# W_out times the gate: made as hi and lo during the second half's projections and kept in DRAM

## The chip, the cores and the metric

The kernel runs on one core of a Trainium2 chip. The metric is the device time of one execution, in microseconds (us). The core's engines work from queues of their own, each in order: TensorE (PE, matrix products), VectorE (DVE), ScalarE (ACT), GpSimd (POOL) and SyncE (SP), which in this kernel issues every transfer between DRAM and on-chip memory (DMA).

## The reference

One layer on a sequence of 2048 rows with 1024 columns, all in float32. A product with `w_in` feeds two groups of heads: 4 heads of 128 with a gated delta rule (DeltaNet, "dn"), and 8 heads of 64 with attention over three dilated windows ("at"). Their outputs, each with its own norm and gate, stand side by side and go through one output product:

```python
mod = jax.nn.silu(c) @ w_mod[layer] + b_mod[layer]
shift, scale, gate = jnp.split(mod, 3, axis=-1)
h = rmsnorm(x, norm_w[layer]) * (1.0 + scale[:, None]) + shift[:, None]
proj = h @ w_in[layer]
...
mix = jnp.concatenate([o_dn, o_at], axis=-1) @ w_out[layer]
x = x + gate[:, None] * mix
return rmsnorm(x, final_norm_w)
```

The gate is one row of 1024 numbers for the whole sequence (there is one `c`), so the kernel multiplies the columns of `w_out` by it once, and not the product.

## The kernel before, in words

**Products.** PE multiplies in a shorter float format (float32r), so each operand is split: `hi` is the value rounded to that format, `lo` the rest. A product is three matmuls, hi by hi, hi by lo and lo by hi; each is recorded at line 149 (L149), and transposes at L154. To make a pair, ACT casts to hi, and POOL or DVE subtracts hi from the value to get lo.

**Stages.** The sequence is worked on in two halves. In each, the projections (16 units of columns of `w_in`, whose hi and lo are kept in the DRAM tiles `ws` after the first use and loaded back as 1 MB transfers, `w_hi<-ws` and `w_lo<-ws`) run on PE, and the DeltaNet scan, the convolutions and rotary terms run beside them. In the second half `gate_row` also works out the gate's row: 16 loads `wg` of 128x512, each added on DVE into `gacc`; the row goes to the DRAM tile `gscr`, which is complete at about 785 us. The projections end at about 1075 us. Then the attention runs, four pairs of heads (p = 0 to 3) with four blocks each, until about 1480 us; the last pair's blocks begin near 1393 us. The rest is the tail of the output product.

**The output product** takes rows 0 to 511 of `w_out` (for the DeltaNet heads' outputs) in three places: `mix_first`, four tiles of 128 rows between the projections and the attention (tiles `mf_oc`, `mf_hi`, `mf_lo`, `mf_x`; the result, `x` plus the product, is stored as `yscr<-mf_x`), and `mix_dn`, the other twelve, as filling between attention blocks (`m_x`). Rows 512 to 1023 (for the attention's outputs) are used by `mix_at`, 16 tiles, in the last pair and the tail.

**The weights of it** are made where they are used. `load_w` loads eight raw pieces of 128x512 and multiplies each by the gate's row, loaded from `gscr`; `split_w` makes hi and lo of them in the tiles of the pool `wp`, which has two slots for hi and two for lo, shared with the projections' `w_hi` and `w_lo`. Two k-tiles of 128 rows fit in one slot, so there are two pairs of tiles for a half of `w_out`, w[0] and w[1]. For the first half this happens in `first_keys`, at the last unit of the second half's projections: all multiplies on DVE (tile `wo_raw`), the gate's row in a piece of `q_lo`. For the second half it is begun in `pair_blocks`, at block 1 of the last pair by the program's numbering (raw pieces in `y_lo`, the gate's row in `y_hi`, DVE and POOL taking turns), and ended by `mix_at`, which waits until all eight are there, and before its first tile also waits for the attention's combined outputs.

**The order.** Generators stand in queues (`side`, `inv`, `dbl`, `scan`, `tail`, `late`, `aux`), and `tick` lets each take one step between the main program's steps; `hop(n)` lets n times 1.1 us of counted PE time go by. Work in `aux`, which holds `gate_row`, is the last in turn. A compiler then orders each engine's queue. The pool `t512` has 9 slots (T5) of 128x512 for small tiles of the projections, `wo_raw`, `z_at` and `wg` among them. The attention's own tiles: `sta` and `stb` are cleared by DVE first, `sm` is the masked scores, `p` the exponents, `pts` their transposes, `va` and `vb` the values, `po` the product with them, `ob` a copy of it by ACT at the end of a block.

## Time and profile before

| | |
|---|---|
| time, median of 3 runs | 1573.51 us (1571.19 to 1579.99) |
| time of the profiled execution | 1573.77 us |
| its span | 1571.5 us |
| granted TensorE clock, mean | 0.974 |
| PE busy | 1439.0 us, 92% |
| DVE busy | 1085.6 us, 69% |
| ACT busy | 655.0 us, 42% |
| POOL busy | 467.7 us, 30% |
| moved by DMA | 252.89 MB, 161 GB/s |

Times in rows count from the span's start. The span is what the trace covers; the execution's own time is 2.3 us longer. A granted clock of 1 is TensorE's upper level, 2.4 GHz. An idle time in square brackets stands before the instruction, with the work whose end released it; a wait for several things is put down to the one that came last, and where that one had long been done it was another. "Landing" is the time from a DMA's issue to its last byte.

### The profile page before, as it was taken

The page shows a single profiled execution, that of the slowest core. Times are in us where ns is not written, and L with a number is a line of the kernel's source. Part 1 is how long each engine was busy: PE and PEld are TensorE (multiplying, and loading weights), DVE is VectorE, ACT ScalarE, POOL GpSimd, SP SyncE. Part 2 cuts the span into 40 slices and gives each one's busy share as a digit, 9 for nine tenths or more (in the row PEclk, how much of TensorE's full clock was granted, in tenths as well). Part 3 has the DMA queues.
Part 4 walks back from the last instruction along what each step waited for, and adds up shares of the span by engine and source line. Part 5 has one row for each costly group of instructions (what it writes and reads, how often), then busy time and mean ns, then how long its engine had stood idle before and what let it go on. Part 6 is the DMA issues. An engine that isn't in the chain of part 4 may idle for free. (4 is left out here: it accounts for less than half of the span.)

```text
span 1571.5 us, 28399 instructions
## 1 busy us (share of the span) xinstructions
PE 1439.0 (92%) x9848; PEld 1162.1 (74%) x9848; DVE 1085.6 (69%) x3395; ACT 655.0 (42%) x1862; POOL 467.7 (30%) x573
## 2 busy tenths in 40 slices
PE   3898899889989879999999999997899999999997
PEld 2686778767767768877878788886677777777776
DVE  6868735775775875687877767435477777888766
ACT  3434224334324663423333243122355554567444
POOL 2324252353362333132141320213122212142243
PEclk9999999999999999999999999999999999999999
DMA  8845551743471652273542515437787747363364
GB/s 243 277 134 190 156 177 58 226 136 125 159 232 47 222 164 88 79 222 113 177 142 88 169 51 156 141 112 238 238 230 209 204 119 233 92 196 103 105 224 161
DMA packets 255183, 252.89 MB, mean 161 GB/s; under 512 B 44864, under 2 KB 196544, under 8 KB 254528
## 3 DMA queue, kind: packets, MB, share of 16 engines
q1 hardware_dynamic: 252592, 242.69, 50.0%
q10 hardware_dynamic: 2448, 8.39, 1.4%
q8 instruction: 78, 1.28, 0.3%
q14 instruction: 65, 0.53, 0.1%
HBM read 160.12 MB, written 90.90 MB: 160 GB/s over the span
## 5 line engine op out<-in xcount | busy, mean ns | idle before, releaser
L149 PE MATMUL ip<-h_hi,w_hi 128*128 128x512 f32 x864 | 353.4, 411 | 2.6 <-DVE gz L690 1.6
L149 PE MATMUL ip<-h_hi,w_lo 128*128 128x512 f32 x864 | 353.8, 411 | 0.0
L149 PE MATMUL ip<-h_lo,w_hi 128*128 128x512 f32 x864 | 351.9, 409 | 0.0
L149 PEld LDWEIGHTS ip<-h_hi,w_hi 128*128 128x128 f32 x864 | 165.3, 191 | 35.0 <-DVE gz L690 2.1
L149 PEld LDWEIGHTS ip<-h_hi,w_lo 128*128 128x128 f32 x864 | 165.5, 192 | 32.1 <-issue 0.2
L149 PEld LDWEIGHTS ip<-h_lo,w_hi 128*128 128x128 f32 x864 | 165.1, 191 | 31.8 <-issue 0.2
L677 DVE SCALAR_TENSOR_TENSOR cv_y<-cv_r,cw,cv_y 128x512 f32<-128x512 f32 x144 | 118.2, 821 | 37.9 <-ACT cv_y L674 34.4
L563 POOL TENSOR_TENSOR w_lo<-w_raw,w_hi 128x512 fp32r<-128x512 f32 x72 | 96.1, 1347 | 123.7 <-ACT w_hi L562 85.3
L1210 DVE CUSTOM_DVE_ANT_0 sm<-s,mask 128x256 f32<-128x256 f32 (+3 forms) x256 | 108.0, 447 | 17.6 <-PE s L149 10.9
L154 PE MATMUL tr<-cst,p 128*128 128x128 f32 x568 | 94.6, 287 | 6.8 <-ACT p L1213 5.3
L1235 DVE COPY pts<-tr 128x512 f32<-128x512 f32 (+1 forms) x120 | 73.1, 616 | 33.8 <-PE tr L154 33.0
L1213 ACT ACTIVATE p<-sm,stb 128x128 f32<-128x128 f32 (+3 forms) x128 | 70.9, 555 | 49.6 <-DVE stb L1210 37.4
L1213 ACT ACTIVATE p<-sm,sta 128x256 f32<-128x256 f32 (+1 forms) x128 | 63.2, 495 | 66.9 <-DVE sta L1210 59.7
L154 PEld LDWEIGHTS tr<-cst,p 128*128 128x128 f32 x568 | 61.8, 142 | 28.6 <-issue 17.1
L149 PE MATMUL ip<-w_hi,h_hi 128*128 128x264 f32 (+1 forms) x256 | 76.2, 298 | 4.8 <-DVE rp L1017 2.1
L791 DVE TENSOR_TENSOR tmp_inv<-xt_inv,blk 128x8 f32<-128x8 f32 (+14 forms) x240 | 73.2, 305 | 5.9
L149 PE MATMUL ip<-w_hi,h_lo 128*128 128x264 f32 (+1 forms) x256 | 75.7, 296 | 0.0
L149 PE MATMUL ip<-w_lo,h_hi 128*128 128x264 f32 (+1 forms) x256 | 75.6, 295 | 0.0
L679 ACT ACTIVATE cv_t<-cv_y 128x512 f32<-128x512 f32 x48 | 30.3, 632 | 86.1 <-DVE cv_y L677 77.0
L562 ACT CAST w_hi<-w_raw 128x512 fp32r<-128x512 f32 x72 | 43.6, 619 | 45.7 <-DMA w_raw<-in_w_in_dram 27.0
L1025 POOL TENSOR_TENSOR rp<-rx,tab 128x512 f32<-128x512 f32 x32 | 42.5, 1339 | 60.8 <-ACT rx L1015 47.1
L1037 POOL TENSOR_TENSOR r_lo<-rpc,r_hi 128x512 fp32r<-128x512 f32 x32 | 42.4, 1325 | 50.6 <-ACT r_hi L1036 28.3
(465 smaller groups left out, 3373.8 us busy)
## 6 DMA issues: line engine op xcount, KB each, us to landing
w_raw<-in_w_in_dram SPq DMA_DIRECT2D x72, 256.0 KB, 3.8
ws<-w_hi SPq DMA_DIRECT2D x15, 1024.0 KB, 5.5
ws<-w_lo SPq DMA_DIRECT2D x15, 1024.0 KB, 7.1
w_hi<-ws SPq DMA_DIRECT2D x15, 1024.0 KB, 5.8
w_lo<-ws SPq DMA_DIRECT2D x15, 1024.0 KB, 7.3
xt<-in_x_dram SPq DMA_DIRECT2D x16, 512.0 KB, 4.8
wm<-in_w_mod_dram SPq DMA_DIRECT2D x32, 256.0 KB, 5.6
tab<-ctab SPq DMA_DIRECT2D x32, 256.0 KB, 3.7
```

Source lines behind the costliest of these rows:

```text
L149: i = self.engine.matmul(ps, lhsT=lhsT, rhs=rhs, **k)
L154: i = self.engine.transpose(*a)
L562: A.copy(hi[:, s, 0:256], raw)
L563: G.tensor_tensor(lo[:, s, 0:256], raw, hi[:, s, 0:256], OP.subtract)
L677: V.scalar_tensor_tensor(y, r[:, n:n + J], cw[:, ti, n:n + 1], y, op0=OP.mult, op1=OP.add)
L679: A.activation(t, y, AF.Tanh)
L791: V.tensor_tensor(tmp[:, :, 0:i + 1], xt[:, :, 0:i + 1], b3[:, i:i + 1, 0:i + 1].to_broadcast([P, 4, i + 1]), OP.mult)
L1025: G.tensor_tensor(p2, xs[1 - ct], tab[1], OP.mult)
L1037: G.tensor_tensor(lo, pc, hi, OP.subtract)
L1210: V.tensor_tensor_reduce(out=sm, in0=pp[hd], in1=masks, scale=-0.125, scalar=BIG, op0=OP.add, op1=OP.min, accum_out=st[:, slot, hd:hd + 1])
L1213: A.activation(pt, sm, AF.Exp, scale=-1.0, bias=st[:, slot, hd:hd + 1], accum_out=st[:, slot, 2 + hd:3 + hd])
L1235: V.tensor_copy(pts[:, 0:kn], pt[:, 0:kn])
```

## The change

`make_w` is put into `aux` behind `gate_row`, so it begins after 785 us. For each of 16 pieces of `w_out` (all of it, both halves) it loads the raw piece and the piece of the gate's row, multiplies on DVE, casts on ACT, subtracts on POOL, and stores hi and lo into eight new DRAM tiles of 1 MB (`wos`). Between these are `hop`s of 4 (WLAG), 4 and 8 (WGAP), and all four of its tiles come from the nine slots of `t512`. `load_w` is now two loads of 1 MB for each pair of tiles. `first_keys` lets the queues step on until the first half is made, issues the loads of w[0], and those of w[1] later; `mix_at` loads the second half. The parts in `first_keys` and `pair_blocks` that loaded, multiplied and split go.

```diff
@@ -60,8 +60,8 @@
 PO = 1
 VD = 1
 VB = 5
-WLAG = 0.5
-GP = (0, 1)
+WLAG = 4.0
+WGAP = 8.0
 CMB = 4
 SMB = 3
 VAB = 3
@@ -272,6 +272,7 @@
     gscr = dram.tile([P, D], F32, name="gscr")
     oscr = [dram.tile([4, P, 4, J], F32, name=f"oscr{i}") for i in range(2)]
     yscr = dram.tile([4, J, D], F32, name="yscr")
+    oscr_w = [[dram.tile([P, 2, D], F32, name=f"wos{i}_{a}") for a in range(2)] for i in range(4)]
 
     def rsqrt(pool, y, a, tag):
 
@@ -1069,29 +1070,36 @@
         drain(aux)
 
 
-    def load_w(raws, ksel, grow, new, lag=0):
-
-        for j in range(8):
-            raw = new(j)
-            c = slice(j % 2 * J, j % 2 * J + J)
-            k = ksel + j // 2
-            dma(raw, w_out[k * P:(k + 1) * P, c])
-            if lag:
-                yield from hop(lag)
-            (G if lag and GP[j % len(GP)] else V).tensor_tensor(raw, raw, grow[:, c], OP.mult)
-            raws.append(raw)
-
-    def split_w(w, raws):
-
-        for i in range(2):
+    made = [0]
+
+    def make_w(pool):
+
+        for i in range(4):
+            for j in range(4):
+                new = lambda nm, dt=F32: pool.tile([P, J], dt, name=nm, tag="t512", bufs=T5)
+                k, c = 2 * i + j // 2, slice(j % 2 * J, j % 2 * J + J)
+                raw, g = new("wo_raw"), new("wo_g")
+                dma(raw, w_out[k * P:(k + 1) * P, c])
+                dma(g, gscr[:, c])
+                yield from hop(WLAG)
+                V.tensor_tensor(raw, raw, g, OP.mult)
+                hi, lo = new("wo_hi", F32R), new("wo_lo", F32R)
+                A.copy(hi, raw)
+                G.tensor_tensor(lo, raw, hi, OP.subtract)
+                yield from hop(WLAG)
+                for a, t in enumerate((hi, lo)):
+                    dma(oscr_w[i][a][:, j // 2, c], t.bitcast(F32))
+                yield from hop(WGAP)
+            made[0] += 1
+
+    def load_w(w, i0):
+
+        for i in range(i0, i0 + 2):
             w.append([flat(wp.tile([P, KT, 264], F32R, name=f"w_{nm}"))[:, 0:2 * D].rearrange("p (k d) -> p k d", k=2)
                       for nm in ("hi", "lo")])
-            for j in range(4):
-                raw = raws[4 * i + j]
-                hi, lo = (w[i][a][:, j // 2, j % 2 * J:j % 2 * J + J] for a in range(2))
-                A.copy(hi, raw)
-                (V if j % 2 else G).tensor_tensor(lo, raw, hi, OP.subtract)
-                yield i
+            for a in range(2):
+                dma(w[-1][a].bitcast(F32), oscr_w[i][a])
+            yield
 
     def class_rows(t, d):
 
@@ -1143,7 +1151,7 @@
 
             yield from mix(hi, lo, oc, w, use)
 
-    w, wa, raws = [], [], []
+    w, wa = [], []
 
 
     def stack(dst, scr, p, hd, step, j0, n):
@@ -1310,8 +1318,6 @@
                 else:
                     ya, yb = ahead["y"] = [hp.tile([P, 4, D], F32, name=f"y_{nm}", tag=f"h_{nm}", bufs=2)
                                            for nm in ("hi", "lo")]
-                    dma(ya[:, 0], gscr)
-                    aux.append(load_w(raws, 4, ya[:, 0], lambda j: yb[:, j // 2, j % 2 * J:j % 2 * J + J], WLAG))
             if blk and p < 3:
                 ahead["load"](blk - 1, blk)
             elif p and blk == 0:
@@ -1454,6 +1460,7 @@
             run(dn_unit(fa, h, js, hs, gts[half], launch, None if half or h else (wv, kqs)))
             if half == 1 and h == 0:
                 aux.append(gate_row(fa))
+                aux.append(make_w(fa))
             if h == 0:
                 ordered[0] = OD == 3
 
@@ -1472,13 +1479,10 @@
         drain(late)
         if jj == 0:
             t = [hp.tile([P, 4, D], F32, name=f"q_{nm}", tag=f"h_{nm}", bufs=2) for nm in ("hi", "lo")]
-            dma(t[1][:, 2], gscr)
-            wr = []
-            for _ in load_w(wr, 0, t[1][:, 2], lambda j: fa.tile([P, J], F32, name="wo_raw", tag="t512", bufs=T5)):
-                pass
-            ahead["w"] = split_w(w, wr)
-            for j in range(4):
-                next(ahead["w"])
+            while made[0] < 2:
+                tick()
+            ahead["w"] = load_w(w, 0)
+            next(ahead["w"])
             ahead["m"] = mix_first(fa)
             next(ahead["m"])
             ahead["q"] = load_q(t, 0, 0)
@@ -1555,9 +1559,7 @@
                 while "y" not in ahead:
                     yield
                 ya, yb = ahead["y"]
-                while len(raws) < 8:
-                    yield
-                yield from split_w(wa, raws)
+                yield from load_w(wa, 2)
                 fw = yb[:, 0]
                 bcast_row(fw, final_w, D)
                 yield from hop(MIXLAG2)
```

How it moves the work, in the compiled order of three places. First DVE, from the end of the projections (`z_at` is the last unit's output, `rs_u` and `rs_o` a norm of the scan) to the attention's first instruction, before:

```order
L1093 TENSOR_TENSOR w_lo<-wo_raw,w_hi 128x512
L282 SCALAR_TENSOR_TENSOR rs_u<-rs_u,so 128x4
L690 SCALAR_TENSOR_TENSOR z_at<-z_t,ip 128x512
L283 SCALAR_TENSOR_TENSOR rs_o<-rs_u,rs_o 128x4
L1093 TENSOR_TENSOR w_lo<-wo_raw,w_hi 128x512
L1141 TENSOR_TENSOR mf_x<-ip,mf_x 128x512 x4
L905 SCALAR_TENSOR_TENSOR oc<-tr,nwz,g 128x512
L1141 TENSOR_TENSOR mf_x<-ip,mf_x 128x512 x4
L1327 MEMSET sta 128x16
```

and after:

```order
L691 SCALAR_TENSOR_TENSOR z_at<-z_t,ip 128x512
L1149 TENSOR_TENSOR mf_x<-ip,mf_x 128x512 x4
L906 SCALAR_TENSOR_TENSOR oc<-tr,nwz,g 128x512
L1149 TENSOR_TENSOR mf_x<-ip,mf_x 128x512 x2
L1085 TENSOR_TENSOR wo_raw<-wo_raw,wo_g 128x512
L1149 TENSOR_TENSOR mf_x<-ip,mf_x 128x512 x2
L1085 TENSOR_TENSOR wo_raw<-wo_raw,wo_g 128x512
L1333 MEMSET sta 128x16
L1334 MEMSET stb 128x16
```

The subtractions are gone, and two of the making's 16 multiplies stand among the `mf_x`, the last of them right ahead of `sta`.

Second, SP's queue at the start of the attention. Before, behind the last two stores of `mf_x` and two pairs of `k` loads (of which the first row here is the end):

```order
L1153 DMA k_lo<-kscr_80 128x1x512
L1188 DMA va<-vscr 32x4x128 x4
L1190 DMA vb<-vscr 128x4x128
L1153 DMA q<-qscr_82 128x1x512 x2
L1188 DMA va<-vscr 32x4x128 x4
L1190 DMA vb<-vscr 128x4x128
```

After, from the last store of `mf_x` on:

```order
L1150 DMA yscr<-mf_x 128x512
L1082 DMA wo_raw<-in_w_out_dram 128x512
L1083 DMA wo_g<-gscr 128x512
L1161 DMA k_hi<-kscr_80 128x1x512
L1161 DMA k_lo<-kscr_80 128x1x512
```

and, behind another pair of `k`:

```order
L1091 DMA wos3_0_130<-wo_hi_11931 128x512
L1091 DMA wos3_1_131<-wo_lo_11932 128x512
L1161 DMA q_11959<-qscr0_82 128x1x512
L1161 DMA q_11960<-qscr0_82 128x1x512
L1161 DMA k_lo_12199<-kscr0_80 128x1x512
L1196 DMA va_11952<-vscr_117 32x4x128 x4
L1198 DMA vb_11953<-vscr_117 128x4x128
```

The load of the last raw piece comes behind the last store of `mf_x`, and the last two stores of the making, of tile `wos3`, ahead of `q`, `va` and `vb`.

Third, SP's queue around the first blocks of the last pair. Before:

```order
L1313 DMA y_hi<-gscr 128x1024
L1153 DMA q<-qscr_83 128x1x512
L1188 DMA va<-vscr 32x4x128 x2
L1078 DMA y_lo<-in_w_out_dram 128x512 x3
L1190 DMA vb<-vscr 128x4x128 x2
L1078 DMA y_lo<-in_w_out_dram 128x512
L1296 DMA oscr_122<-a_oc 512x1x128
L1250 DMA agz<-zscr 128x4x128
L1078 DMA y_lo<-in_w_out_dram 128x512 x2
L1253 DMA sscr<-sta 128x16
```

After, some two blocks earlier in the program, at the end of the pair before:

```order
L1101 DMA w_lo<-wos_1_129 128x2048
L1258 DMA agz<-zscr 128x4x128
L1304 DMA oscr_122<-a_oc 512x1x128
L1554 DMA yscr<-m_x 128x512
L1196 DMA va<-vscr 32x4x128 x4
L1261 DMA sscr<-sta 128x16
L1101 DMA w_hi<-wos_0_128 128x2048
L1161 DMA q<-qscr_83 128x1x512 x2
L1263 DMA stc<-sscr 32x4x4 x4
L1101 DMA w_hi<-wos_0_130 128x2048
L1101 DMA w_lo<-wos_1_131 128x2048
```

The eight loads of 256 KB and the gate's row became four loads of 1 MB, and these moved ahead by about two blocks. PE's order in the second half's projections is as before; twelve matmuls of `mix_at` moved from the tail in among the last pair's blocks.

## Rows read from the trace of the kernel before

**Rows 1.** Stretches: length, PE, PEld, DVE, ACT, POOL busy; clock, DMA share, GB/s.

```profile
783.00:1060.00 277.00, 272.38 (x2026) 222.00 (x2025) 174.23 (x549) 86.43 (x261) 67.65 (x110) 1.00 0.38 122
1070.00:1080.00 10.00, 4.18 (x19) 2.81 (x17) 9.83 (x17) 4.35 (x10) 4.88 (x5) 0.91 0.78 255
1080.00:1090.00 10.00, 8.48 (x27) 6.53 (x28) 5.09 (x11) 1.62 (x3) 4.65 (x4) 0.74 0.57 158
1380.00:1400.00 20.00, 19.39 (x183) 15.06 (x181) 18.94 (x67) 14.23 (x42) 7.86 (x8) 1.00 0.63 190
```

**Rows 2.** Tile wg, 600 to 800 us: ns min/median/max; DVE's idle time.

```profile
L337 DVE SCALAR_TENSOR_TENSOR gacc<-wg,sc,gacc x14: 698/750/1732, 682.6 to 764.9; 128x512 f32<-128x512 f32 x14
...
  DMA wg<-in_w_mod_dram: 5.2, 3
```

**Rows 3.** PE's timeline at the boundary: start us, us, instruction.

```profile
1074.51 0.40 PE L149 MATMUL ip<-h_lo,w_hi 128*128 128x512 f32 x1
1074.74 0.40 PE L149 MATMUL ip<-h_hi,w_lo 128*128 128x512 f32 x1
...
1083.01 0.63 PE L149 MATMUL ip<-w_hi,mf_lo 128*128 128x512 f32 x1
1083.44 0.63 PE L149 MATMUL ip<-w_hi,mf_hi 128*128 128x512 f32 x1
```

**Rows 4.** PE's waits, 1055 to 1125 us: us in total, times, longest.

```profile
PE ip L149 <- DVE rs_u L282: 5.6, 1, 5.6
...
PE po L149 <- DMA va<-vscr: 2.0, 1, 2.0
PE s L149 <- DVE sta L1327: 1.5, 1, 1.5
...
PE sc L149 <- ACT y L138: 1.0, 1, 1.0
```

**Rows 5.** DVE's timeline: start us, us, instruction, [idle before it <- releaser].

```profile
1081.66 0.68 DVE L690 SCALAR_TENSOR_TENSOR z_at<-z_t,ip 128x512 f32<-128x512 f32 x1
...
1085.80 0.69 DVE L1141 TENSOR_TENSOR mf_x<-ip,mf_x 128x512 f32<-128x512 f32 x1 [2.03 <-PE ip L149]
...
1112.48 0.69 DVE L1141 TENSOR_TENSOR mf_x<-ip,mf_x 128x512 f32<-128x512 f32 x1 [2.93 <-DMA mf_x<-in_x_dram]
1113.12 0.07 DVE L1327 MEMSET sta<- 128x16 f32 x1
```

**Rows 6.** The page: DMA issues, KB each, median us to landing.

```profile
w_hi<-ws SPq DMA_DIRECT2D x15, 1024.0 KB, 5.8
w_lo<-ws SPq DMA_DIRECT2D x15, 1024.0 KB, 7.3
```

**Rows 7.** Tile wo_raw: ns min/median/max, first and last start; landing of its DMAs.

```profile
L1081 DVE TENSOR_TENSOR wo_raw<-wo_raw,q_lo x8: 676/686/1770, 1067.3 to 1075.8; 128x512 f32<-128x512 f32 x8
...
L1093 POOL TENSOR_TENSOR w_lo<-wo_raw,w_hi x4: 1262/1398/1622, 1068.7 to 1081.9; 128x512 fp32r<-128x512 f32 x4
...
DMA to landing us min/median/max: 3.8/4.9/5.8
```

**Rows 8.** The timeline of SP's queue: start us, us, DMA, count.

```profile
1116.11 2.02 SPq L1188 DMA_DIRECT2D va<-vscr  x4
```

**Rows 9.** PE's timeline: the first products with va.

```profile
1122.38 1.96 PE L149 MATMUL po<-pts,va 128*64 128x128 f32 x18 [1.97 <-DMA va<-vscr]
```

**Rows 10.** One stretch, tile y_lo alone: DVE, ACT, POOL busy (instructions).

```profile
1388.00:1412.00 24.00, 5.81 (x6) 4.64 (x8) 10.81 (x8) 0.87 0.76 240
```

**Rows 11.** ACT's timeline: the copies that end the blocks of the last pair.

```profile
1393.28 0.56 ACT L1368 COPY ob<-po 128x512 f32<-128x512 f32 x1
...
1412.62 0.59 ACT L1368 COPY ob<-po 128x512 f32<-128x512 f32 x1 [1.15 <-PE po L149]
...
1429.21 0.58 ACT L1368 COPY ob<-po 128x512 f32<-128x512 f32 x1
```

**Rows 12.** DMA from 1048 to 1122 us: packets, bytes, mean.

```profile
DMA packets 13472, 15.81 MB, mean 214 GB/s; under 512 B 977, under 2 KB 7631, under 8 KB 13467
```

## The prediction

> **What bounds the kernel now.** I read the busy shares first (the table above: TensorE, PE, far ahead of VectorE, DVE), so work on other engines counts only where PE then waits; then the stretches, then the waits inside three of them. By stretches [rows 1], the second half's projections, 783 to 1060 us, leave PE 4.6 of 277 us idle, while DVE is idle for 103. The boundary to the attention, 1070 to 1080, is turned round: DVE 9.83 of 10 us busy, PE 4.18. At 1380 to 1400, in the attention, both are nearly full (19.39 and 18.94 of 20). The change takes work out of the two tight places and puts it into the loose one; what it leaves at the tight ones decides.
>
> **The loose stretch.** Each of 16 steps loads a raw 128x512 piece and a piece of the gate row, multiplies on DVE, casts on ScalarE (ACT), subtracts on GpSimd (POOL), and stores hi and lo. Engines serve their queues in order, so a multiply whose piece is late holds all that is behind it on DVE, and a store whose POOL result is late holds all later loads on SyncE's queue (SP). The nearest row is the gate row's own sum: 16 loads of the same size, each consumed by a DVE instruction and DVE idle for them 5.2 us in 3 waits [rows 2]. A step here has two such loads, so 10.4 us if in proportion and if all of it reached PE; nothing if DVE's 103 idle us swallow it. I take a quarter, **+2.6 (0 to +10.4)**: in the old run PE idled only 4.6 us in a stretch where DVE idled 103. The 16 casts and subtractions lie under PE's work there: should that cover fail, DVE's 16 multiplies at 0.69 us would be 11 us.
>
> A row to weigh: a gacc of one form takes 0.75 us at the median and 1.73 at most [rows 2]. The Trainium skill (SBUF — State Buffer, Who interferes with whom) says that a DVE instruction with two inputs in SBUF contends with a GpSimd instruction that reads it, and one of them blocks; the change puts all 16 subtractions on GpSimd. By that the worst is 16 times 0.98 = 15.7 us of DVE time more, an estimate from that row; with a quarter of it on PE, as above, the sum at the end would be 1582 instead of 1578. The row's median of 0.75 shows the long form to be the exception, so I leave it out of the sum and give it 0.03 of A's chance of slower.
>
> **The boundary up to the last mf_x.** The last projection matmul ends at 1075.1 [rows 3]; PE had waited 1.0 us for an ACT y, and then waits 5.6 us for a PSUM bank [rows 4]. The profile calls the releaser rs_u, but the banks are freed by the last two z_at on DVE, the later at 1081.66 [rows 5], queued behind multiplies of W_out and w_lo subtractions. With these gone, the 1.0 us goes. The 5.6 does not go whole: the second pair of loaded weights, w[1], reuses the slot of the last projection's weights, so its hi is issued only at that unit's end, T, and its lo behind the store of the last z_at (I take T+2.1: two z_at of 0.68 and a store issue). A 1 MB load of this form lands in 5.8 (hi) and 7.3 us (lo) [rows 6], so T+5.8 and T+9.4. PE can run 12 matmuls on w[0] before, at 0.43 us spacing at the lower clock level or 0.23 at the full one [rows 3]; at 1080 to 1090 the granted clock is 0.74 [rows 1]; then it waits for w[1]. Its other 12 end at T+12.2 to T+14.6, while in the old run the two mf_x of the first tile start with 1085.80 [rows 5], T+10.7. So the first tile is about even, the earlier T gives 1, and a little comes from lighter DVE and ACT: **-1.5**. Lower end -3, if the wait is filled and the ten slow-clock matmuls (10 x 0.20 us) become fast. Upper end +4: lo issued only at T+6.5, where the last z_at was before.
>
> The loads of 1 MB deserve a word. The row gives 5.8 and 7.3 us. The Trainium skill (SBUF — State Buffer, The DMA setup-cost knee) has a fixed 2 us and 436 GB/s, hence 4.4 us for 1 MB and 2.6 for 256 KB, an estimate from its fit, and advises the largest transfers, which speaks for this change. By it w[1] would be 2.9 us earlier and the whole sum lower by that, 1575; the trace has 256 KB landing in 4.9 here [rows 7], so I stay with the rows.
>
> **The start of the attention.** Here I see the loss. The steps of the making do not all end before the projections: in the changed order the last two multiplies stand among the first W_out tiles, the two before them in the last head's scan. The last one's raw load is on SP right behind the store of the last mf_x, its multiply right before the memset of sta, the attention's first DVE instruction, and its store of lo stands before q and va. In the old trace the last mf_x starts at 1112.48, and the memset follows at 1113.12 without a gap [rows 5]. Now call Y the end of the last mf_x: the load is issued at Y+0.5, lands 3.8 to 5.8 us later [rows 7], and takes 0.69 to be multiplied: sta comes at Y+5.0 to Y+7.0 instead of Y. PE waits for sta already (1.5 us, [rows 4]). Then the cast on ACT and the POOL subtraction (1.3 to 1.6 us, [rows 7]) hold the store of lo to about Y+8.5, and behind it stand q, a k_lo and four va. The old SP put the four va out from 1116.11 on [rows 8], some 3 us after Y, and PE, which waited 2.0 us for them [rows 4], began with them at 1122.38 [rows 9]: Y+9.2, 4.3 us after the last was issued. The new SP needs from Y+8.5 some 2 us for the store, q and k, 2.0 for the va, and with 4.3 as before the po matmuls start near Y+16.8: 7.6 later. The two delays overlap. Scores and transposes of the first block fill little of it, because they depend on the DVE that is late too. **+6.5 (+5.0 to +12)**: the upper end is the va delay with landings of 5.8 throughout and with k and q late as well.
>
> **Last pair of heads.** Before, eight raw pieces are loaded, multiplied, cast and subtracted during the blocks around 1388 to 1412; on DVE this is 5.81 us [rows 10]. Its first block ends at 1412.62, 19.34 us after 1393.28; the next, without such work, takes 16.59 [rows 11]. The work removed is thus worth 2.75: **-2.8**, lower end -5.8 (DVE is full, all of it counts), upper end 0 (see D). What it leaves is the DVE's own attention work, which is then the last.
> In its place four loads of 1 MB now stand on SP some 30 us earlier, in front of q and va loads of the pair before. A load behind one can be late by its 7.3 us [rows 6] less the 3 or so that it takes alone: **+1 (0 to +4)**. Where PE has scores of another block in hand, it hides this.
> **Tail.** Twelve of the W_out matmuls of the tail get in among the attention's, 12 x 0.23 = 2.8 us if PE had idle time for them there; I take half, **-1.5 (-2.8 to 0)**: PE has few gaps at 1380 to 1400.
>
> **The sum**: 2.6 - 1.5 + 6.5 - 2.8 + 1.0 - 1.5 = +4.3. The profiled execution took 1573.77 us, 0.26 from the median of the runs, 1573.51; so 1573.8 + 4.3 = 1578.1, I say **1578**.
>
> **Rivals.**
> A, the forecast, 1571 to 1586, chance 0.50.
> B, faster: the old wait before W_out, DVE's load in the last pair and the tail pay in full (-3, -5.8, -2.8), the loose stretch costs nothing, and the start of the attention is late only by part of what the order shows, +1.5, because PE had W_out tiles to finish meanwhile: 1573.8 - 10.1 = 1563.7. For it speaks the 5.6 us gap and DVE's full 10 us; against it, that the multiply before sta waits for a load issued after the last tile. 0.13.
> C, slower: traffic. Between 1048 and 1122 the queue moves 15.81 MB at a mean of 214 GB/s [rows 12]; at 1070 to 1080, where the transfers crowd, 255 [rows 1]. The change brings 4 MB of loaded weights and four steps of 1 MB here, and takes 2.5 MB away: +5.5 MB. At 255 GB/s that is 21.6 us, against a room of 74 us x (255 - 214) = 3.0 MB or 11.9 us. So 9.7 us are not hidden, and mf_x's operands, k and va land late by that: 1578.1 + 9.7 = 1587.8. It decides from the point at which the added bytes exceed that room; below it the transfers only shift. 0.27.
> D, the last pair does not get faster: the 19.34 us of its first block come from something else (a wait on q, the slower clock), and the added loads cost their 1 us: 1578 + 2.8 = 1581. 0.10.
>
> **How the numbers follow.** A change of 0.5%, 7.9 us, is about what a measurement of this kernel can tell from none: faster is below 1565.6, slower above 1581.4. A gives 0.01 faster, 0.40 same, 0.09 slower; B 0.11 and 0.02 same; C 0.25 slower and 0.02 same; D 0.07 same and 0.03 slower. Sums: faster 0.12, same 0.51, slower 0.37. The range leaves out a tenth at each end: 1566 cuts most of B, 1591 the upper part of C. A's own range is 1571 to 1586.
>
> **What would show it.** Right: DVE idle for a DMA of wo_raw for about 5 us right before the first sta, and PE waiting at the first po for va longer than 2.0 us; W_out's first 12 matmuls soon after the last projection, then a wait of PE for w_hi or w_lo in place of the 5.6 us; the last pair's first block near 16.6 us; PE's idle time at 783 to 1060 within 4.6 plus some 3 us. Wrong: wo_raw landing before the last mf_x is done (then B), DVE or PE waiting for x, k or DRAM weights all through the first tiles (then C), or a first block still at 19 us (D). A PE idle time of over 10 us more in the loose stretch would refute my first term.

## The result, and the profile after

The changed kernel takes 1590.59 us (median of four runs, 1589.48 to 1591.08) against 1574.51 before: a ratio of 1.0108, 95% interval 1.0078 to 1.0137. It is slower, by some 16 us where the forecast was 4.3. The profiled execution takes 1589.48 us, its span 1587.7.

Where the 16 us are. The table takes the start of the same instruction in both traces; a stage is longer by the difference of its two ends. It begins with a unit at 766 us, before the change does anything (the making's first load is issued at 773 us, ahead of the 785 given above, since the half of the gate's row that it needs is stored first): up to there the profiled executions of this study, whose program is the same so far, already differ by -5.8 to +2.6 us from the one before, so only differences from that point on are used.

| stage | before, us | after, longer by | forecast |
|---|---|---|---|
| from 766 to the last projection matmul | 309.2 | +6.5 | +2.6 |
| to the end of the last `mf_x` | 38.0 | +0.6 | -1.5 |
| to `sta` | 0 | +7.5 | +6.5 for this and the next two |
| to the first `po` | 9.3 | +1.0 | |
| to the end of the attention's second block | 38.0 | +5.3 | |
| to the beginning of the last pair | 232.9 | -0.3 | +1.0 |
| its first block | 19.3 | -4.5 | -2.8 |
| its other blocks | 60.9 | +6.2 | -1.5 for this and the next |
| the tail | 94.2 | -5.0 | |
| sum | | +17.4 | +4.3 |

The tail's row ends at the issue of the last store. The earlier part was 1.1 us shorter, so that store comes 16.3 us later. First PE's waits from 1055 to 1160 us after the change (total in us, times, longest), which answer to [rows 4]:

```profile
PE s L149 <- DVE sta L1218: 4.3, 1, 4.3
PE po L149 <- DMA va<-vscr: 3.3, 1, 3.3
PE tr L154 <- POOL o L900: 3.1, 1, 3.1
PE s L149 <- DVE mf_x L1149: 2.9, 1, 2.9
PE ip L149 <- DVE mf_x L1149: 2.3, 1, 2.3
PE ip L149 <- DMA w_lo<-wos: 2.1, 1, 2.1
```

The old wait of 5.6 us before the first W_out matmul is gone; in its place stand 3.1 for a part of the scan and 2.1 for the loaded `w_lo`. The two rows that were 1.5 and 2.0 are now 2.9 plus 4.3, and 3.3. DVE's timeline shows why (start, us, instruction, idle time before it and its releaser), to be read against [rows 5]:

```profile
1117.89 1.29 DVE L1149 TENSOR_TENSOR mf_x<-ip,mf_x 128x512 f32<-128x512 f32 x2 [5.38 <-DMA mf_x<-in_x_dram]
1125.93 0.69 DVE L1085 TENSOR_TENSOR wo_raw<-wo_raw,wo_g 128x512 f32<-128x512 f32 x1 [6.75 <-DMA wo_g<-gscr]
1126.58 0.07 DVE L1333 MEMSET sta<- 128x16 f32 x1
```

`sta` came at once behind the last `mf_x` before; now DVE stands 6.75 us for a piece of the gate's row, multiplies, and only then clears `sta`. SP's queue of the same time, to [rows 8]:

```profile
1120.67 0.62 SPq L1082 DMA_DIRECT2D wo_raw<-in_w_out_dram  x1
1121.35 0.65 SPq L1083 DMA_DIRECT2D wo_g<-gscr  x1
...
1128.71 0.33 SPq L1091 DMA_DIRECT2D wos<-wo_lo  x1
...
1130.96 2.02 SPq L1196 DMA_DIRECT2D va<-vscr  x4
```

The loads of the last step are issued 1.5 us behind the last `mf_x`, its store of lo 8.0 later, and `va` behind that; PE's first product with `va` follows at 1136.90, 17.7 us behind the last `mf_x`, where it was 9.2 [rows 9]. Then the stretches (length, PE, PEld, DVE, ACT, POOL busy; granted clock, DMA share, GB/s), to [rows 1]:

```profile
783.00:1060.00 277.00, 267.52 (x1955) 216.71 (x1955) 183.60 (x553) 90.32 (x267) 84.89 (x122) 0.99 0.52 169
1120.00:1130.00 10.00, 5.66 (x25) 4.86 (x24) 3.75 (x20) 3.28 (x13) 1.27 (x1) 0.50 0.87 295
1130.00:1140.00 10.00, 6.08 (x42) 5.18 (x40) 2.42 (x15) 3.47 (x15) 1.22 (x2) 0.50 0.80 229
1140.00:1150.00 10.00, 10.00 (x41) 7.83 (x40) 2.65 (x14) 4.58 (x16) 1.28 (x1) 0.51 0.45 142
```

The loose stretch leaves PE 9.5 us idle instead of 4.6. And from 1120 to 1150, after and during the waits, TensorE's granted clock is 0.50, the lower of its two levels. In the last of these three rows PE waits for nothing and is busy all the time, yet does 41 matmuls. The stretch from the first `po` to the end of the second block, before and after:

```profile
1122.40:1160.40 38.00, 37.58 (x275) 30.20 (x275) 18.65 (x70) 17.22 (x54) 8.79 (x9) 0.96 0.79 229
```

```profile
1136.90:1180.30 43.40, 41.67 (x274) 32.57 (x275) 22.54 (x85) 18.88 (x61) 9.87 (x10) 0.85 0.68 203
```

At full clock both would take 36 to 37 us (an estimate: length times mean clock). So by these figures the +5.3 behind the first `po` is the clock, and no term of the forecast held it.

Last, the ends of the blocks of the last pair, to [rows 11] (ACT's timeline; the first row is the end of the block before):

```profile
1412.87 0.56 ACT L1374 COPY ob<-po 128x512 f32<-128x512 f32 x1
...
1427.67 0.59 ACT L1374 COPY ob<-po 128x512 f32<-128x512 f32 x1 [0.55 <-PE po L149]
...
1443.92 0.56 ACT L1374 COPY ob<-po 128x512 f32<-128x512 f32 x1
```

Its first block takes 14.80 us, where it took 19.34: the work that was taken out there was on the path.

### The profile page after: what moved, and what is told of

Its sections match the earlier page's. It is cut to its first block, busy times and chain, and to the rows that moved or that the text cites. A ratio compares the mean times of both kernels' runs of the same rounds, so it can differ in the third digit from the quotient of the medians.

```text
span 1587.7 us, 28537 instructions
## 1 busy us (share of the span) xinstructions
PE 1448.8 (91%) x9848; PEld 1166.1 (73%) x9848; DVE 1086.5 (68%) x3391; ACT 654.7 (41%) x1862; POOL 471.0 (30%) x577
## 5 line engine op out<-in xcount | busy, mean ns | idle before, releaser
L1218 DVE CUSTOM_DVE_ANT_0 sm<-s,mask 128x256 f32<-128x256 f32 (+3 forms) x256 | 107.5, 447 | 22.4 <-PE s L149 16.6
L792 DVE TENSOR_TENSOR tmp_inv<-xt_inv,blk 128x8 f32<-128x8 f32 (+14 forms) x240 | 79.1, 330 | 6.1
```

What stands on the lines that cost most here:

```text
L792: V.tensor_tensor(tmp[:, :, 0:i + 1], xt[:, :, 0:i + 1], b3[:, i:i + 1, 0:i + 1].to_broadcast([P, 4, i + 1]), OP.mult)
L1218: V.tensor_tensor_reduce(out=sm, in0=pp[hd], in1=masks, scale=-0.125, scalar=BIG, op0=OP.add, op1=OP.min, accum_out=st[:, slot, hd:hd + 1])
```

## The experiments

Two theories to begin with. **Theory 1**: the loss is made where the last steps of the making stand, ahead of the attention. **Theory 2**, rival C: the way through DRAM costs by its bytes. Ratios are to the kernel before, measured beside it on the same chip, with their 95% interval.

**WGAP 4.** The steps follow each other sooner, so that all are done before the last scan.

```diff
-WGAP = 8.0
+WGAP = 4.0
```

> The changed kernel with WGAP 4 instead of 8 and nothing else: the 16 steps follow each other sooner, so that the last multiply and the last stores stand ahead of the last scan of the projections and none in the first W_out tiles or at the start of the attention. Theory 1 (the loss is where the last two steps stand: DVE's wait ahead of sta, the stores ahead of q and va, and the lower clock after these waits): of the changed kernel's lateness the 20.8 us that stand at the end of the second pair's blocks fall to the 6 or 7 us of the loose stretch, the last pair and the tail still give 4.6 back, so 1574 to 1577 us, ratio to the kernel before 1.000 to 1.002. Theory 2 (the bytes through DRAM, and weights loaded in 1 MB pieces at the boundary, cost wherever the steps stand): still above 1585, ratio over 1.007.

Ratio 1.0012 (0.9996 to 1.0028), 1574.43 us: no difference from the kernel before can be told, and the 16 us are gone. From the end of the projections on, the last `mf_x` is 4.1 us earlier, `sta` comes at once (DVE's timeline):

```profile
1112.20 0.69 DVE L1149 TENSOR_TENSOR mf_x<-ip,mf_x 128x512 f32<-128x512 f32 x1 [2.06 <-PE ip L149]
1112.84 0.07 DVE L1333 MEMSET sta<- 128x16 f32 x1
```

and PE waits for the loaded weights (its waits, 1055 to 1160 us) 3.6 us in place of 5.6:

```profile
PE ip L149 <- DMA w_lo<-wos: 2.6, 1, 2.6
...
PE ip L149 <- DMA w_hi<-wos: 1.0, 1, 1.0
```

The loose stretch stays 7.5 us longer and the last pair and the tail give 3.2 back. Theory 1 holds for the start of the attention; the gains of 4.1 and 3.2 us are there, and the loose stretch takes them back. The 4.1 is the largest of its kind: in the eleven other traces of this study in which the first half goes through DRAM and no step of the making stands behind the projections (below), the last `mf_x` is 1.7 to 3.5 us earlier, and 1.4 where the boundary was left as it was.

**WGAP 10**, the opposite: three steps between the last `mf_x` and the attention.

> The changed kernel with WGAP 10 instead of 8: now three steps stand between the last mf_x and the attention, each one's loads on SP behind the stores of the one before, and all ahead of va. The wait is thus trebled: one step takes load (4.9 us), multiply (0.7), cast (0.6) and subtraction (1.3), some 7.5 us. Theory 1 (the chain of load, multiply and store ahead of sta and va sets the start of the attention): sta late by 20 to 25 us against the last mf_x, instead of 7.5; PE's lower clock lasts as long; the whole at 1602 to 1612. Theory 2 (the bytes through DRAM): the same bytes, so 1588 to 1593 as the changed kernel.

Ratio 1.0270 (1.0233 to 1.0307), 1610.64 us. That is 41.8 us above the kernel before beside it (1568.85), more than the 28 to 38 that theory 1 gave, counted from 1573.8. DVE's timeline:

```profile
1124.23 0.69 DVE L1149 TENSOR_TENSOR mf_x<-ip,mf_x 128x512 f32<-128x512 f32 x1 [0.60 <-PE ip L149]
1130.56 0.69 DVE L1085 TENSOR_TENSOR wo_raw<-wo_raw,wo_g 128x512 f32<-128x512 f32 x1 [5.64 <-DMA wo_g<-gscr]
1137.83 0.69 DVE L1085 TENSOR_TENSOR wo_raw<-wo_raw,wo_g 128x512 f32<-128x512 f32 x1 [6.58 <-DMA wo_g<-gscr]
1145.56 0.69 DVE L1085 TENSOR_TENSOR wo_raw<-wo_raw,wo_g 128x512 f32<-128x512 f32 x1 [7.03 <-DMA wo_g<-gscr]
1146.20 0.07 DVE L1333 MEMSET sta<- 128x16 f32 x1
```

Three steps in a row, each 6.3 to 7.7 us, since the next one's load stands on SP behind the store of the one before: `sta` is 21.3 us late. PE's longest wait (1055 to 1175 us) is

```profile
PE s L149 <- DVE sta L1218: 19.9, 1, 19.9
```

The lower clock did not reach as far behind this wait as I expected: it was 0.50 from 1132 to 1152 us, most of which is the wait itself, and the stretch from the first `po` (1155.65) to the second block's end is 2.3 us longer, not 5.3. So here the price of the clock did not grow with the wait; it was paid on the work that stood in the slow stretch. The loose stretch of this trace is 14.0 us longer than before, 7.5 more than with WGAP 8; this is of the size of the excess, and no run explains it.

The bytes of the whole program are the same as with WGAP 8. In the 45 us behind the projections' last matmul, DMA moves as much in the good case as in the bad ones (changed kernel; WGAP 4; WGAP 10):

```profile
DMA packets 7446, 12.51 MB, mean 278 GB/s; under 512 B 647, under 2 KB 2695, under 8 KB 7188
```

```profile
DMA packets 8770, 12.72 MB, mean 283 GB/s; under 512 B 755, under 2 KB 4288, under 8 KB 8512
```

```profile
DMA packets 7875, 13.27 MB, mean 295 GB/s; under 512 B 704, under 2 KB 2752, under 8 KB 7616
```

So it is the place in the queues and not the traffic that makes the 16 us; rival C's 1587.8 was close by its number alone.

**WGAP 7**, between: the last step ahead of the last two `mf_x`.

> The changed kernel with WGAP 7: the last step's loads come ahead of the last four mf_x's stores, its multiply ahead of the last two mf_x, and its stores right behind the last store of mf_x, still ahead of va. The bytes at the boundary are nearly those of the changed kernel, the chain behind the last mf_x is gone. Theory 1: the attention starts within 2 us of the last mf_x as in the kernel before, and the time is that of WGAP 4 within 3 us, 1573 to 1578. Theory 2 (traffic of the steps at the boundary): between the two, 1580 to 1586.

Ratio 1.0082 (1.0050 to 1.0113), 1580.80 us: the time that theory 2 gave, not theory 1. The bytes do not tell this kernel from WGAP 4 (12.34 MB in the 45 us behind the projections' last matmul, against 12.72), and the trace shows the same kind of chain as before at two other places (DVE's timeline):

```profile
1084.21 0.69 DVE L1085 TENSOR_TENSOR wo_raw<-wo_raw,wo_g 128x512 f32<-128x512 f32 x1 [1.97 <-DMA wo_g<-gscr]
1086.57 0.69 DVE L691 SCALAR_TENSOR_TENSOR z_at<-z_t,ip 128x512 f32<-128x512 f32 x1
...
1120.64 0.69 DVE L1085 TENSOR_TENSOR wo_raw<-wo_raw,wo_g 128x512 f32<-128x512 f32 x1 [4.86 <-DMA wo_g<-gscr]
1121.36 0.69 DVE L1149 TENSOR_TENSOR mf_x<-ip,mf_x 128x512 f32<-128x512 f32 x1
```

The last step but one waits for its gate's piece ahead of the scan's last norm and the last `z_at`, and behind the store of that `z_at` stands the load of `w_lo`: the first `mf_x` comes 2.9 us later, against the projections' end, than with WGAP 4. The last step's gate piece is loaded behind two stores of `mf_x`, and the last two `mf_x` wait behind its multiply. Together their end is 5.9 us later than with WGAP 4; `sta` follows at once. Behind it another 5.7 us are lost: the first `po` comes 2.0 us later than in the kernel before and the next two blocks take 3.7 more, with a granted clock of 0.50 from 1130 to 1147 us. I had looked at the raw piece's place on SP and not at that of the gate's. That these chains make all of the loss is read from the trace; no run parts them from a later landing of `x`, for which DVE waits 8.3 us ahead of the fifth `mf_x` here and 6.9 with WGAP 4.

**The multiply on GpSimd**, WGAP 8.

```diff
-                V.tensor_tensor(raw, raw, g, OP.mult)
+                G.tensor_tensor(raw, raw, g, OP.mult)
```

> The changed kernel with the multiply of each step on GpSimd instead of DVE; the steps stand where they did, SP's order of loads and stores is nearly the same. It parts DVE's waits for the pieces from the waits of SP's queue for the stores. Theory 1 as put (both matter): sta no longer late by 7 us, but va still behind the last stores, and these later by some 0.7 us since GpSimd's multiply takes 1.3; the first po late by 10 to 13 us instead of 14.5; the loose stretch falls from 6.7 us to about 2, if DVE's waits for the gate row's pieces (10.5 us in 5 waits) were its cause. Together 1581 to 1585. If va alone decides the start and the loose stretch has another cause: 1589 to 1591. If DVE alone decides: 1574 to 1577.

Ratio 1.0152 (1.0129 to 1.0175), 1594.03 us, slower still and above all three of my ranges. `sta` is on time again, but the first `po` comes 9.1 us late, against 8.5 in the changed kernel. ACT's timeline shows who took DVE's place:

```profile
1134.26 0.62 ACT L1087 CAST wo_hi<-wo_raw 128x512 fp32r<-128x512 f32 x1 [14.35 <-POOL wo_raw L1085]
1134.79 0.40 ACT L1221 ACTIVATE p<-sm,sta 128x128 f32<-128x128 f32 x1
```

and SP's queue:

```profile
1136.25 0.33 SPq L1091 DMA_DIRECT2D wos<-wo_lo  x1
...
1138.50 2.02 SPq L1196 DMA_DIRECT2D va<-vscr  x4
```

The cast stands on ACT right ahead of the attention's first exponent, and the store ahead of `va`. One late load holds three queues: DVE ahead of `sta`, ACT ahead of `p`, SP ahead of `va`. To free one of them is not enough. What makes this kernel slower still is the loose stretch, 13.1 us longer instead of 6.5.

**The multiply on GpSimd, WGAP 4.**

> Both edits: WGAP 4, so all steps are done before the boundary, and the multiply on GpSimd. Theory 1 with DVE's waits as the cause of the loose stretch's loss: 1569 to 1572, since about 2 us stay in the loose stretch and the last pair and the tail give 4.6 back. If the loose stretch's loss has another cause (the DMA traffic, the nine slots of small tiles): 1574 to 1577, as the other kernel with WGAP 4. If GpSimd becomes late for the rotary terms and the scan: above 1577.

Ratio 1.0056 (1.0034 to 1.0078), 1580.36 us. The attention starts on time, but the loose stretch is longer by 12.4 us instead of 7.5. That DVE's wait for the pieces were the cause of the loose stretch's loss falls with this run in its simple form: the wait only moved, to GpSimd (38 us in nine waits for `wo_g`), and ACT waits for the product as before (17.6 us in ten waits, 16.6 in nine with WGAP 4).

**One half of W_out at a time.** In one kernel only the first half goes through DRAM:

```diff
-        for i in range(4):
+        for i in range(2):
```

with the second half made in the last pair as before.

> Only the first half of W_out goes through DRAM (8 steps, hops as in the changed kernel); the second half is made in the last pair as in the kernel before. Eight steps end long before the boundary. Theory 1: about half of the loose stretch's 6.7 us, the attention's start as in the kernel before, no gain in the last pair: 1575 to 1578. At the boundary it shows what loading w[0] and w[1] is worth by itself, since no step of the making stands there: the last mf_x relative to the last projection within 1.5 us of the kernel before by my sum, earlier by 3 or more if the 5.6 us wait was the bound. Theory 2 (1 MB loads at the boundary cost): over 1583.

Ratio 1.0013 (0.9997 to 1.0030), 1574.44 us. The loose stretch is 3.4 us longer, the last `mf_x` 3.0 earlier against the projections' end, the last pair as before. In the other only the second half does (`range(2, 4)`), and the first is made at the boundary as before:

> Only the second half of W_out goes through DRAM (8 steps with the hops of the changed kernel), the first half is made at the boundary as in the kernel before. Eight steps should cost the loose stretch 3 to 4 us, as with only the first half through DRAM (3.4); the boundary is as before, 5.6 us of wait included; the last pair and the tail give back 3 to 5 us (4.5 at the block that ends the loading, given partly away by W_out matmuls that come among the last blocks). Together 1571 to 1575, no difference that could be told. If the last pair's gain was rather from the boundary: 1576 to 1578.

Ratio 1.0018 (1.0001 to 1.0036), 1572.11 us. Its loose stretch is 5.8 longer, more than I expected; the last pair and the tail give 3.1 back; and the old wait is there as it was (PE's waits):

```profile
PE ip L149 <- DVE rs_u L283: 5.6, 1, 5.6
```

So the last pair's gain belongs to the second half and the boundary's to the first, some 3 us each, and each half costs as much or more in the loose stretch, 3.4 and 5.8. The boundary's figure is the less certain: with the old boundary in place it was 1.4 us shorter all the same.

**What the loose stretch loses.** All of these have the twelve hops a step of WGAP 4, and each changes one part of a step. The number to compare is how late PE's matmul of 1000 us is, against the same at 755: 8.9 us with WGAP 4. Each is one execution: the two kernels with eight steps, alike there but for the pieces, differ by 0.9 (4.7 and 5.6), and by 2.4 over the whole stretch (3.4 and 5.8). Whole times of these kernels lie within 0.6% of each other, and their intervals mostly overlap, so the argument is on this number.

Loads and stores alone (the pieces are stored as they landed):

> The kernel with WGAP 4 without the multiply, the cast and the subtraction of the 16 steps: the two loads of each step are stored as they landed, so W_out times the gate is not made, the loads and stores alone run. In the kernel with WGAP 4 the loose stretch, from the gate's unit at 766 us to the end of the projections, was 7.5 us longer than in the kernel before. If the loads and stores (traffic, and SP's queue held by waits) cause that: still 6 to 8 us longer. If the instructions on DVE, ACT and POOL and what waits behind them cause it: 0 to 2 us longer, and the whole at about 1568 to 1570.

0.0 us late at 1000 us. But to the end of the projections, which is the measure of my expectation, the stretch is 4.7 us longer, between its two cases: behind 1000 us a load of projection weights comes late (PE's waits, 766 to 1076 us):

```profile
PE ip L149 <- DMA w_lo<-ws: 4.1, 2, 3.2
```

Ratio 1.0008 (0.9986 to 1.0030): without any of the making's arithmetic the whole is no faster than before.

With the multiply:

> The kernel with WGAP 4 with the loads, the multiplies on DVE and two stores a step, but without the casts and subtractions (what is stored is the product and the gate's row, so W_out's hi and lo are not made). Without any of the three the loose stretch was late by less than 1 us up to 1000 us, against 8 us with all three. If the multiplies and DVE's waits for their pieces (10.9 us in ten waits with WGAP 4) cause it: 5 to 8 us late by 1000 us. If the casts on ACT, which wait for the multiplies and hold ACT's own queue (16.6 us in nine waits), cause it: under 2.5 us.

2.9 us late, between my two cases; ratio 1.0037 (1.0020 to 1.0055). With multiply and cast, hi stored twice:

> The kernel with WGAP 4 without the subtraction (hi is stored twice, lo is not made): three slots a step, DVE's multiply and ACT's cast as they were. If ACT's cast with its wait is the cause: 6 to 8 us late at 990 us, as with all three. If the subtraction, which holds GpSimd for 50 us of waits for the casts, is: about 3 us, as with the multiply alone. If the ring is: between, 4 to 6.

3.0 us late; ratio 0.9977 (0.9957 to 0.9997), by 0.2% the one kernel that was faster, without the subtraction. With all three, cast and subtraction on 8 columns only:

> The kernel with WGAP 4 with cast and subtraction on 8 of the 512 columns only, and the product and the gate's piece stored (so W_out's hi and lo are not made): four slots a step, ACT still waits for DVE's multiply and GpSimd for ACT's cast, but their work is nearly nothing. If slots or waits between the engines cause the loose stretch's loss: 6 to 8 us late at 990 us. If the length of the cast and the subtraction does: about 3 us, as with the multiply alone.

5.4 us late, again between; ratio 1.0007 (0.9984 to 1.0031). So up to 1000 us the subtraction, with the slot and the store of its result, brings about 6 of the 8.9, and with hardly any length still about 2.5. Three kernels that do all the work, placed otherwise. The subtraction on DVE:

> The kernel with WGAP 4 with the subtraction on DVE instead of GpSimd. With the multiply moved to GpSimd the loose stretch grew from 7.5 to 12.4 us (WGAP 4) and from 6.5 to 13.1 (WGAP 8), though DVE no longer waited for the pieces: so it seems to be GpSimd's queue that PE feels, by the rotary terms and the scan's parts behind it. If so, the stretch falls to 2 to 5 us longer than before, and the time to 1569 to 1572. If DVE's queue is what counts (11 us more work there, and POOL's gain not felt): 9 to 12 us longer, 1576 to 1579.

7.6 us late, between the two; ratio 1.0011 (0.9990 to 1.0032). The cast on DVE:

> The kernel with WGAP 4 with the cast on DVE, right behind the multiply, so that ACT takes no part and its queue never waits for a piece; DVE has some 10 us more to do in the loose stretch. If ACT's waits for the multiplies (16.6 us in nine waits) cause the loose stretch's loss: it falls from 7.5 to 2 to 4 us, and the time to 1568 to 1571. If DVE's queue causes it: 8 to 11 us, 1574 to 1578.

8.9 us late, as I put it for DVE's queue; ratio 1.0027 (1.0008 to 1.0047). Three slots of `t512` a step instead of four:

> The kernel with WGAP 4 with lo written over the gate's piece, so a step takes three of the nine slots of small tiles instead of four; the instructions and the transfers are the same. The loose stretch was late by 8 us at 990 us with four slots a step, whichever engine did the work, and by 3 and 1 us in the two kernels with two slots a step (that also did less work). If the ring of nine slots is the cause: 3 to 5 us late at 990 us, the time 1568 to 1571. If the work itself is: still 7 to 9 us.

9.2 us late; ratio 1.0028 (1.0004 to 1.0053): not the ring. Two kernels that deal the hops out otherwise. Later multiplies:

> The kernel with WGAP 4 with the hops dealt out otherwise, 8, 4 and 0 instead of 4, 4 and 4: each multiply comes 4.4 us of PE time later behind its loads, in the same total. DVE's waits for the gate row's pieces, 10.9 us in ten waits in the kernel with WGAP 4, should nearly go. If these waits cause the loose stretch's loss: it falls from 7.5 to 2 to 4 us. If not: it stays within 1.5 us of 7.5, and the time with it.

8.5 us late; ratio 1.0030 (1.0010 to 1.0050). This run tells less than it should have: DVE still waited 13.8 us for `wo_g`, since its loads had not come earlier on SP by as much as the multiply came later. Later subtractions:

```diff
                 A.copy(hi, raw)
+                yield from hop(WLAG)
                 G.tensor_tensor(lo, raw, hi, OP.subtract)
```

> The kernel with WGAP 4 with the subtraction issued 4 hops (4.4 us of PE time) behind the cast instead of right behind it, and no gap behind the stores: the same instructions and transfers, the same 12 hops a step. GpSimd's waits for the casts (50 us in eight waits, up to 14.4, with WGAP 4) should mostly go. If these waits cause the part of the loose stretch's loss that the subtraction brings: 3 to 5.5 us late at 1000 us instead of 8.9, and the time at 0.996 to 0.999 of the kernel before. If the length of GpSimd's work causes it: 8 to 9 us late, and no faster than WGAP 4.

11.1 us late, above both cases; ratio 1.0029 (1.0011 to 1.0046). POOL's waits for the cast, which were (WGAP 4, 766 to 1075 us)

```profile
POOL wo_lo L1088 <- ACT wo_hi L1087: 50.2, 8, 14.4
```

became

```profile
POOL wo_lo L1089 <- ACT wo_hi L1087: 27.4, 3, 16.4
```

with no gain, though half of the waits stayed. To the end of the projections (against 766 us) the same kernels compare otherwise:

| kernel | late at 1000 us | late at the projections' end | PE's waits for weights from `ws`, 766 to 1076 us |
|---|---|---|---|
| WGAP 4 | 8.9 | 7.5 | 0 |
| loads and stores alone | 0.0 | 4.7 | 4.1 |
| with the multiply | 2.9 | 5.9 | 2.9 |
| with multiply and cast | 3.0 | 2.7 | 1.1 |
| cast and subtraction on 8 columns | 5.4 | 9.5 | 3.4 |
| subtraction on DVE | 7.6 | 7.2 | 0.8 |
| cast on DVE | 8.9 | 8.2 | 0.5 |
| three slots | 9.2 | 8.3 | 0.2 |
| later multiplies | 8.5 | 9.0 | 1.4 |
| later subtractions | 11.1 | 10.8 | 0.7 |

Over the whole stretch the parts do not add up. The kernels with less arithmetic lose part of it behind 1000 us, to weights of the projections that land late, so the way through DRAM is not free there, and the 6 us of the subtraction are a reading up to 1000 us alone. With the subtraction on either engine PE waits longer for tiles of the scan (its waits, 770 to 1076 us; before, then WGAP 4):

```profile
PE g L149 <- DVE w L138: 1.3, 1, 1.3
...
PE tr L154 <- DVE oc L905: 0.5, 1, 0.5
```

```profile
PE g L149 <- DVE w L138: 4.5, 4, 3.3
PE tr L154 <- DVE oc L906: 2.8, 2, 1.9
```

No run points to GpSimd's time, its wait for the cast, DVE's wait or the ring alone as the cause. One rival has no run of its own: SP's queue, where each store of lo waits for the subtraction (11.5 us in eleven waits with WGAP 4) and all that is behind it waits too; with the subtraction on DVE these waits are 5.2 us in six, and the stretch is hardly better, which speaks against it. Each of these edits also moves other instructions in the queues. What exactly makes the loss stays open. None of the kernels that compute all of it is faster than the kernel before.

## Why the prediction was wrong

**The direction and the place were right, the size was not.** The chain that I saw in the order (load behind the last store of `mf_x`, multiply ahead of `sta`, store ahead of `va`) is the loss: without it the change costs nothing that can be told (ratio 1.0012), with three of it in a row 1.0270, of which `sta` alone is 21.3 us. My most likely case, no more than 0.5%, did not come. That 1590.59 still lies just inside the range, 1566 to 1591, is luck: I had set that end for rival C, the traffic.

**The start of the attention** was the term that failed most. Its working held fairly well up to the first `po`: loads issued at Y+1.5 (I said 0.5), `sta` at Y+7.4 (5.0 to 7.0), the store of lo at Y+9.5 (8.5), `po` at Y+17.7 (16.8). That is +8.5 against a value of +6.5 (the working itself gave 7.6). The step that failed is that the sum ends there, and what comes after stood in it at nothing: PE's granted clock fell to 0.50 during the waits and stayed there until 1150, and PE, by then busy without a gap, did its work at half the pace. To the second block's end this is another +5.3, the largest single miss. I had counted such a stretch at the boundary (the ten slow matmuls of [rows 3]) as something to win, and not asked what new waits right ahead of the attention would do to the clock behind them. I also overlooked a third queue, ACT, on which the cast stands ahead of the first exponent.

**The loose stretch**, +6.5 to +7.5 instead of +2.6. DVE's own wait for the pieces came out at the end that I had worked out for it in proportion (10.5 us in 5 waits from 783 to the end of the projections, against 10.4). The quarter of it that I took for PE was not far off up to 1000 us, where the kernel with loads and multiplies alone is 2.9 us late; to the end of the projections it is 5.9. The step that failed is that I priced nothing else: the casts and subtractions, put wholly under PE's work, bring some 6 us up to 1000 us, and the loads and stores by themselves 4.7 to the end. DVE's 103 idle us, which I had set against the whole, do not help PE where it waits for one operand of the scan. I had named the cover and priced its failure at 11 us, but gave it no share.

**The boundary**, -1.5 forecast, +0.6 found. With no step left in it, it is -1.7 to -4.1 in twelve traces: the gain that I had forecast was there, with PE's first twelve W_out matmuls at once and then a wait for the loaded `w_hi` and `w_lo` (3.6 us with WGAP 4) in place of the 5.6. The number did not follow from my working, though: its T+12.2 to T+14.6 against T+10.7 is a first tile 1.5 to 3.9 us later, which I called about even. With WGAP 4 the first `mf_x` came at T+9.8, as the weights were there sooner (PE goes on with `w_lo` at T+8.0, where I had T+9.4). The step that failed is that I let only the last step of the making cost something, and took the ones before it, at the end of the scan and among the `mf_x`, for free. In the changed kernel DVE waits 1.5 us for a piece of the gate's row ahead of the last `z_at`, behind whose store the load of `w_lo` stands, and the first `mf_x` comes 3.3 us later against the projections' end than with WGAP 4. With WGAP 7 two such places cost 5.9 us.

**Last pair and tail**, -2.8 + 1.0 - 1.5 = -3.3 forecast, -0.3 - 4.5 + 6.2 - 5.0 = -3.6 found. The first block won 4.5 us, its work having weighed 1.7 more than the difference of two blocks showed. The other blocks are 6.2 longer and the tail 5.0 shorter. Of the 6.2 the twelve moved W_out matmuls explain about 3: with later multiplies and with WGAP 10, which have them too, the other blocks are 2.9 and 3.1 us longer. In the changed kernel the third block also ran at a granted clock of 0.87 (1.00 in these two). So the matmuls found no idle PE there, where I had counted on half of it. The loads of 1 MB in front of `q` and `va` cost nothing that shows (-0.3). Rival D is refuted.

**The rules weighed.** The Trainium skill's fit (SBUF — State Buffer, The DMA setup-cost knee) gave 4.4 us for 1 MB, an estimate; the loads of the made weights landed in 5.4 (hi) and 6.5 us (lo) with WGAP 4, nearer to the rows that I stayed with (5.8 and 7.3). The Trainium skill's rule on DVE and GpSimd (SBUF — State Buffer, Who interferes with whom) would, by the row that I weighed it with, have had the multiplies at up to 1.73 us; of the 16 the median was 0.69 and the longest 1.08 (1.45 with WGAP 4), so the length of the multiplies is not where the loose stretch lost.

**Rival B** came nearest to being true in the kernels with WGAP 4, where its condition, no step at the start of the attention, is met; even there the loose stretch takes its gain back.

## What to carry to other kernels

When work is moved ahead so that it can hide, look in the compiled order for its last piece, not its first: a step that starts with a load holds every in-order queue on which one of its later instructions stands, and the load itself may be issued behind a store that closes the stage before. Price such a wait on the path as the whole chain from load to store on all queues, and look at which work will stand behind it when PE has idled: at the lower clock that work took 5.3 us more here. And give a cover a price in the likeliest sum, if a serial chain runs beside it: average idle time of an engine does not hide a wait for one operand.

## What the runs showed of the hardware that was not expected

After PE's waits at the start of the attention (2.9 us, then 4.3, with scores at the lower level between) the granted clock was 0.50 for three slices of 10 us, the last of which had PE busy throughout; in the kernel with WGAP 4, whose waits there are 0.8 and 1.9 us, no slice of 10 us from 1100 to 1140 was below 0.83. With WGAP 10, behind a wait of 19.9 us, the lower level lasted about 20 us, most of it the wait itself. And profiled executions with the same program up to 766 us differed there by up to 8 us, -5.8 to +2.6 against the one before, so that changes of a few us could be read only from a point inside the trace on.
